# Scaling softmax probabilities: one broadcast product for two heads in place of two per-head products

## The chip, the cores and the metric

The kernel runs on one core of a Trainium2 chip. Its engines are TensorE (PE in the profile; PEld is its weight load), VectorE (DVE), ScalarE (ACT), GpSimd (POOL) and SyncE (SP, which here issues the DMAs). The metric is the device time of one execution in microseconds. Before the change the median of three runs is 2153.99 us, the lowest 2150.99, the highest 2158.84.

## The reference

One layer of a hybrid decoder runs over a prompt of 2048 tokens and a sample group of 8 x 8 tokens, with shared weights. What matters here is the attention of the prompt: 8 query heads on 2 key/value heads (so 4 heads in a group), head size 64, a causal window of 128, and a learned logit per head (the sink) that only enters the denominator.

```python
s = jnp.einsum('...qhgd,...shd->...hgqs', q, k) * (HEAD_DIM ** -0.5)
s = jnp.where(mask, s, NEG)
m = jnp.maximum(jnp.max(s, axis=-1, keepdims=True), sink)
e = jnp.exp(s - m)
pr = e / (jnp.sum(e, axis=-1, keepdims=True) + jnp.exp(sink - m))
return jnp.einsum('...hgqs,...shd->...qhgd', pr.astype(v.dtype), v)
```

The rest of the layer is an input projection, a pooling mixer, an output projection, a feed-forward block of width 4096 and a gated embedding. The change touches only the division that makes `pr`.

## The kernel before

The prompt is cut into 16 tiles of 128 tokens, and the sample group is one more tile of 64 (t = -1). The program has four parts, one after the other on TensorE: the attention part (projection, attention, pooling per tile), the output projection, the up projection, and the down projection with the gate. The attention part ends some 410 us into the span.

In the attention part, one loop over t weaves four generators in an order that is written out as a string of letters: `f` is `front` of tile t+1 (three projections, PSUM tiles `kvps`, `qps` and `ups`, then rotary embedding and transposes `trk` and `trq` of keys and queries), `a` is `attention` of tile t, `p` is `pooling` of tile t (transpose `tru`, products `pq`), `l` is `finish` of tile t-1 (`pss`), and `e` carries side work. At the last tile, t = 15, there is no next front; there `e` is `mixed.first`, which loads the output weights `wo` and starts the output projection (PSUM tile `pab`) so that TensorE has something between the steps of the last attention.

This weaving is the program order. The compiling layer then orders each engine's instructions anew from the dependencies and its own modelled durations (`schedule_with_timeline_sim=True`), unless a line holds an instruction to program order. So an edit of one instruction's kind or length can also move others, on all engines. Within an engine, instructions run in the order that results; an instruction that waits holds up everything behind it on its engine.

For a tile, `attention` (L491) goes through the two groups g of four heads:

- TensorE makes the scores of each head (`sc`, L505 and L506, two products each, 256 keys wide; 128 for tile 0).
- VectorE adds the mask, takes the running minimum of the negated scores and evicts them to `pr` (L509), a head at a time.
- ScalarE takes the exponential of each head in place, with its sum (L520).
- A short chain on four columns makes the denominators and their reciprocals `es` (L529 VectorE, L530 ScalarE, L531 and L532 VectorE).
- Four products scale the four heads in place: heads 0 and 2 on VectorE (L537), heads 1 and 3 on ScalarE (L535). Each takes one head of 128 x 256 and a per-partition scalar `es[:, hh:hh+1]`.
- TensorE transposes the four scaled heads of each block of 128 keys into one PSUM bank (`trp`, L547, four transposes). ScalarE casts the bank to `pt` (L549), VectorE writes the remainder of the cast beside it (L130, tile `pt`), and TensorE multiplies both with the values (`po`, L557 and L558).
- VectorE folds the two halves of `po` into `mix` (L560 and L561) and ScalarE squares them (L564).

The PSUM pool `tr` has two buffers. All of `trp`, `trk`, `trq` and `tru` take turns in them, and a transpose can start only when the reader of the tile two turns earlier is done. For `trp` the last reader is the remainder on VectorE, for the others a copy or cast on ScalarE (L460, L471, L581).

Of the kernel before, what the change touches and what calls it, by code (L numbers as in the profile page):

```python
# [14 lines left out]
ALU = mybir.AluOpType  # L15
PSUM = bass.MemoryType.PSUM

P = 128
# [70 lines left out]
def trunk(ctx: ExitStack, tc: tile.TileContext, i: dict, o: dict):  # L89
    nc = tc.nc  # L90
    V, A, G, T, SY = nc.vector, nc.scalar, nc.gpsimd, nc.tensor, nc.sync
# [37 lines left out]
    def lo_of(out, full, hi, eng=V):  # L129
        eng.tensor_tensor(out=out, in0=full, in1=hi.bitcast(F32), op=ALU.subtract)  # L130
# [143 lines left out]
    with ExitStack() as sa:  # L274
# [8 lines left out]
        op = sa.enter_context(tc.tile_pool(name="op", bufs=2, space=PSUM))  # L283
# [207 lines left out]
        def attention(t, kp, qT, mix, sq):  # L491

            nk = 1 if t == 0 else 2
            k0 = 256 - nk * P
            nkey = nk * P
            prs = []
            for g in range(2):
                pr = over.pool.tile([P, 4, 256], F32, tag="pr", bufs=2, name="pr")
                nm = over.pool.tile([P, 4], F32, tag="nm", bufs=2, name="nm")
                sm = over.pool.tile([P, 4], F32, tag="sm", bufs=2, name="sm")  # L500
                for h2 in range(2):
                    sc = scp.tile([P, 2, 256], F32, tag="sc", name="sc")
                    for e in range(2):
                        h = g * 4 + h2 * 2 + e
                        T.matmul(sc[:, e, :nkey], qT[:, h], kp[:, g * 2, k0:], start=True, stop=False)  # L505
                        T.matmul(sc[:, e, :nkey], qT[:, h], kp[:, g * 2 + 1, k0:], start=False, stop=True)  # L506
                    for e in range(2):
                        hh = h2 * 2 + e
                        V.tensor_tensor_reduce(  # L509
                            out=pr[:, hh, :nkey],  # L510
                            in0=sc[:, e, :nkey],
                            in1=ct[:, C_MASK + k0 : C_MASK + 256],
                            scale=-(HD**-0.5),
                            scalar=nsink[:, g * 4 + hh : g * 4 + hh + 1],
                            op0=ALU.add,
                            op1=ALU.min,
                            accum_out=nm[:, hh : hh + 1],
                        )
                for hh in range(4):
                    A.activation(  # L520
                        out=pr[:, hh, :nkey],
                        in_=pr[:, hh, :nkey],
                        func=AF.Exp,
                        scale=-1.0,
                        bias=nm[:, hh : hh + 1],
                        accum_out=sm[:, hh : hh + 1],
                    )
                es = over.pool.tile([P, 4], F32, tag="es", bufs=2, name="es")
                V.tensor_tensor(out=es, in0=nm, in1=sinkb[:, g * 4 : g * 4 + 4], op=ALU.add)  # L529
                A.activation(out=es, in_=es, func=AF.Exp)  # L530
                V.tensor_tensor(out=es, in0=es, in1=sm, op=ALU.add)  # L531
                V.reciprocal(es, es)  # L532
                for hh in range(4):
                    if hh % 2:
                        A.mul(out=pr[:, hh, :nkey], in_=pr[:, hh, :nkey], mul=es[:, hh : hh + 1])  # L535
                    else:
                        V.tensor_scalar_mul(pr[:, hh, :nkey], pr[:, hh, :nkey], es[:, hh : hh + 1])  # L537
                prs.append(pr)
                yield
            part = over.pool.tile([P, 4, P], F32, tag="part", bufs=1, name="part")  # L540
            for g in range(2):
                pr = prs[g]
                pts = []
                for kb in range(nk):
                    ps = tr.tile([P, 4, P], F32, tag="tr", name="trp")
                    for hh in range(4):
                        T.transpose(ps[:, hh, :], pr[:, hh, kb * P : (kb + 1) * P], ident)  # L547
                    pt = over.pool.tile([P, 2, 4, P], F32R, tag="pt", bufs=3, name="pt")
                    A.copy(out=pt[:, 0], in_=ps)  # L549
                    lo_of(pt[:, 1], ps, pt[:, 0])  # L550
                    pts.append(pt)
                yield

                po = op.tile([P, 4, P], F32, tag="o", name="po")
                for kb in range(nk):
                    vp = vps[(t - nk + 1 + kb) % 4]
                    T.matmul(po, vp[:, 2 * g : 2 * g + 2].rearrange("p a d -> p (a d)"), pts[kb][:, 0], start=kb == 0, stop=False)  # L557
                    T.matmul(po, vp[:, 4 + g : 6 + g].rearrange("p a d -> p (a d)"), pts[kb][:, 1], start=False, stop=kb == nk - 1)  # L558
                own, other = slice(g * HD, g * HD + HD), slice(HD - g * HD, 2 * HD - g * HD)
                V.tensor_copy(part[own], po[other])  # L560
                V.tensor_tensor(out=mix[own, 0:4, :], in0=po[own], in1=part[own], op=ALU.add)  # L561
                if g == 0:
                    yield
            A.activation(out=sq[:, 0:4, :], in_=mix[:, 0:4, :], func=AF.Square)  # L564
# [219 lines left out]
        for t in range(-1, NT):  # L784
            kr, vr, qr, u, kp, qT = res[t]
            if t + 1 < NT and t >= 0:
                split_head(t + 1)
            mix = pa.tile([P, 8, P], F32, tag="mix", bufs=2, name="mix")
            sq = pa.tile([P, 8, P], F32, tag="sq", bufs=2, name="sq")
            if t + 2 < NT:  # L790
                heads[t + 2] = head(t + 2)
            f = front(t + 1, *heads[t + 1], res[t + 1]) if t + 1 < NT else iter(())
            p = pooling(t, u, mix, sq)
            if t < 0:
                a = sample_attention(kr, vr, qr, mix, sq)
                for c in ORDER0.split():
                    next({"a": a, "p": p, "f": f}[c], None)
                run(a, p, finish(t, mix, sq))
                over_s.__exit__(None, None, None)
                over.pool = sa.enter_context(tc.tile_pool(name="over_p", bufs=1, side="right", reuse_waits="tile"))  # L800
                run(f)
            else:
                e = split_w_out((t - 3) % 4, (t - 3) // 4) if 3 <= t < 11 else iter(())
                if t == NT - 1:
                    sw.close()
                    s2 = ctx.enter_context(ExitStack())
                    mixed = Mixed(s2)
                    bank = sw.enter_context(tc.tile_pool(name="first", bufs=2, space=PSUM, reuse_waits="tile"))
                    e = mixed.first(bank)
                order = {NT - 2: ORDER1, NT - 1: ORDER2}.get(t, ORDERW if 3 <= t < 11 else ORDER)  # L810
                weave(order, a=attention(t, kp, qT, mix, sq), p=p, f=f, l=last, e=e)
                last = finish(t, mix, sq)
# [700 lines left out]
```

## Time and profile before

| | |
|---|---|
| runs (three) | 2150.99 to 2158.84 us, median 2153.99 |
| profiled execution | 2156.64 us, its span 2154.9 us |
| busy share of the span | PE 99%, PEld 87%, DVE 73%, ACT 44%, POOL 27% |
| mean granted TensorE clock | 0.996 |
| scaling on VectorE (L537) | 64 instructions, 26.1 us busy |
| scaling on ScalarE (L535) | 64 instructions, 28.6 us busy |

The profile comes from one execution. A row of the grouped view gives the line, the engine, the operation, what it writes and reads, how often, the busy time in us and the mean duration in ns, and then how long its engine stood idle just before it and who ended that. The waits view sums who waited for whom. In the view by windows each row is a stretch: its bounds, its length, and for PE, PEld, DVE, ACT and POOL the busy us with the number of instructions, then the granted TensorE clock, the DMA share and GB/s. A row of the timeline begins with the start in us and the time taken; two instructions that follow each other on an engine can overlap, so what one costs its engine in a stream is the distance between starts.

### The profile page before, as it was taken

To read this page: it belongs to the slowest core of one execution; us is meant where nothing else is said; L and a number is where in the kernel's file an instruction comes from. 1 tells how busy PE (TensorE), PEld (TensorE's weight loads), DVE (VectorE), ACT (ScalarE), POOL (GpSimd) and SP (SyncE) were. 2 spreads that over 40 slices of the span, in tenths; PEclk is the share of its full clock that TensorE was granted. 3 is DMA by queue.
4 is the path that set the end of the run, shared out by engine and by line. 5 is a ranking of instruction groups with operands and counts; after the bars stand their busy time and mean duration, and the time that the engine had idled before them with its cause. 6 is when DMAs were issued, how large, how long until landed. Compare 5 with 4: busy or idle time off the path is not lost. (4 is left out here: it accounts for less than half of the span.)

```text
span 2154.9 us, 31214 instructions
## 1 busy us (share of the span) xinstructions
PE 2129.8 (99%) x11439; PEld 1882.8 (87%) x11439; DVE 1573.8 (73%) x2719; ACT 956.8 (44%) x1864; POOL 576.3 (27%) x643
## 2 busy tenths in 40 slices
PE   8999999999999999999999999999999999999999
PEld 6888888788889999999999988788888888888887
DVE  6899888876688777555755566788888888876553
ACT  5676666545455445444544455233232233232221
POOL 2334343343440000000000035534534544300000
PEclk9999999999999999999999999999999999999999
DMA  7552122768789668666766532231231222342211
GB/s 221 176 174 92 63 70 67 264 220 249 230 259 322 223 217 273 208 191 190 225 197 189 164 111 92 97 101 49 92 99 53 97 91 72 107 138 83 89 54 40
DMA packets 310007, 320.43 MB, mean 149 GB/s; under 512 B 79775, under 2 KB 257247, under 8 KB 302654
## 3 DMA queue, kind: packets, MB, share of 16 engines
q1 hardware_dynamic: 309854, 318.44, 46.7%
q8 instruction: 90, 1.47, 0.3%
q14 instruction: 63, 0.52, 0.1%
HBM read 217.17 MB, written 102.51 MB: 148 GB/s over the span
## 5 line engine op out<-in xcount | busy, mean ns | idle before, releaser
L1278 DVE TENSOR_TENSOR z<-dn,z 128x512 f32<-128x512 f32 x416 | 277.8, 684 | 78.0 <-PE dn L1270 70.1
L130 DVE TENSOR_TENSOR g<-raw,g 128x512 fp32r<-128x512 f32 x336 | 226.8, 694 | 88.9 <-ACT g L207 88.2
L1052 PE MATMUL up<-e,g 128*128 128x352 f32 x832 | 269.5, 324 | 6.0 <-ACT snap L1059 5.8
L1053 PE MATMUL up<-e,g 128*128 128x352 f32 x832 | 267.9, 322 | 0.0
L1054 PE MATMUL up<-e,g 128*128 128x352 f32 x832 | 264.3, 323 | 0.0
L1217 POOL TENSOR_TENSOR raws<-raws 128x1024 f32<-128x1024 f32 x32 | 84.0, 2635 | 617.6 <-DVE wr L130 408.4
L207 ACT CAST g<-raw 128x512 fp32r<-128x512 f32 x336 | 203.8, 623 | 97.4 <-PE up L1054 77.4
L1268 PE MATMUL dn<-wr,ms 128*128 128x512 f32 x512 | 199.3, 390 | 1.5 <-DVE z L1278 1.5
L1269 PE MATMUL dn<-wr,ms 128*128 128x512 f32 x512 | 199.2, 389 | 0.0
L1270 PE MATMUL dn<-wr,ms 128*128 128x512 f32 x512 | 198.2, 389 | 0.0
L1052 PEld LDWEIGHTS up<-e,g 128*128 128x128 f32 x832 | 156.6, 188 | 7.2 <-ACT snap L1059 6.6
L1053 PEld LDWEIGHTS up<-e,g 128*128 128x128 f32 x832 | 157.4, 189 | 0.1
L1054 PEld LDWEIGHTS up<-e,g 128*128 128x128 f32 x832 | 156.0, 189 | 0.0
L1066 DVE TENSOR_TENSOR t<-up,snap 128x352 f32<-128x352 f32 x144 | 71.2, 520 | 115.4 <-ACT snap L1059 100.0
L207 ACT CAST m<-fr 128x512 fp32r<-128x512 f32 (+1 forms) x128 | 65.4, 514 | 194.2 <-PE dn L1270 172.5
L1268 PE MATMUL dn<-wr,m 128*128 128x512 f32 x384 | 149.5, 389 | 1.7 <-DVE z L1278 1.7
L1269 PE MATMUL dn<-wr,m 128*128 128x512 f32 x384 | 149.4, 389 | 0.0
L1270 PE MATMUL dn<-wr,m 128*128 128x512 f32 x384 | 149.3, 389 | 0.0
L848 POOL TENSOR_TENSOR s<-fr 128x256 f32<-128x256 f32 x64 | 54.1, 845 | 308.3 <-DVE ms L130 241.7
L1059 ACT COPY snap<-up 128x352 f32<-128x352 f32 x144 | 61.0, 454 | 165.6 <-PE up L1054 165.6
L207 ACT CAST wr<-raws 128x1024 fp32r<-128x1024 f32 x66 | 69.1, 1050 | 116.5 <-PE dn L1270 57.8
L1268 PEld LDWEIGHTS dn<-wr,ms 128*128 128x128 f32 x512 | 96.1, 188 | 22.1 <-issue 1.9
(279 smaller groups left out, 5725.8 us busy)
## 6 DMA issues: line engine op xcount, KB each, us to landing
raw<-in_w_up_dram SPq DMA_DIRECT2D x160, 256.0 KB, 4.4
raw<-upt SPq DMA_DIRECT2D x32, 1024.0 KB, 7.8
fr<-ffd SPq DMA_DIRECT2D x64, 512.0 KB, 3.5
ffd<-r SPq DMA_DIRECT2D x96, 256.0 KB, 2.9
upt<-raw SPq DMA_DIRECT2D x16, 1024.0 KB, 8.5
raws<-in_w_down_dram SPq DMA_DIRECT2D x32, 512.0 KB, 5.4
sp<-hfd SPq DMA_DIRECT2D x21, 704.0 KB, 6.6
xt<-in_x_t_dram SPq DMA_DIRECT2D x16, 512.0 KB, 5.7
```

The source lines that it names most:

```text
L130: eng.tensor_tensor(out=out, in0=full, in1=hi.bitcast(F32), op=ALU.subtract)
L207: copy(out=dst[:, 0], in_=src)
L1052: T.matmul(ps, l[0], r[0], start=st, stop=False, skip_group_check=not fresh)
L1053: T.matmul(ps, l[0], r[1], start=False, stop=False, skip_group_check=not fresh)
L1054: T.matmul(ps, l[1], r[0], start=False, stop=c == 3, skip_group_check=not fresh)
L1059: A.copy(out=s, in_=ps)
L1066: V.tensor_tensor(out=t, in0=ps, in1=s, op=ALU.add)
L1217: G.tensor_tensor(out=t, in0=x, in1=y, op=ALU.subtract)
L1268: T.matmul(ps, l[0], r[0], start=fresh and j == 0, stop=False, skip_group_check=not fresh)
L1269: T.matmul(ps, l[0], r[1], start=False, stop=False, skip_group_check=not fresh)
L1270: T.matmul(ps, l[1], r[0], start=False, stop=j == 1, skip_group_check=not fresh)
L1278: V.tensor_tensor(out=z, in0=ps, in1=z, op=ALU.add)
```

## The change

The loop over four heads with alternating engines is replaced. Heads 0 and 1 are scaled by a single elementwise product on VectorE, of a 128 x 2 x 256 block with the two reciprocals broadcast along the keys. Heads 2 and 3 are scaled on ScalarE, each as before with a per-partition scalar.

```diff
                 V.reciprocal(es, es)
-                for hh in range(4):
-                    if hh % 2:
-                        A.mul(out=pr[:, hh, :nkey], in_=pr[:, hh, :nkey], mul=es[:, hh : hh + 1])
-                    else:
-                        V.tensor_scalar_mul(pr[:, hh, :nkey], pr[:, hh, :nkey], es[:, hh : hh + 1])
+                some = pr[:, 0:2, :nkey]
+                V.tensor_tensor(out=some, in0=some, in1=es[:, 0:2].unsqueeze(2).to_broadcast([P, 2, nkey]), op=ALU.mult)
+                for hh in range(2, 4):
+                    A.mul(out=pr[:, hh, :nkey], in_=pr[:, hh, :nkey], mul=es[:, hh : hh + 1])
                 prs.append(pr)
```

The changed file is one line shorter, so from the transposes on each line number is one less than before (L547 becomes L546, and so on); the new product is L534 and the products on ScalarE are L536.

The order of the instructions is moved on every engine from tile 0 on, to the middle of the output projection; behind that it stands as before. Three places are shown.

VectorE, tile 4, second group of heads, before (`es` are the reciprocals, `qr` and `rb` the rotary embedding of tile 5's queries):

```order
L532 RECIPROCAL es<-es 128x4
L406 TENSOR_TENSOR qr<-qps,cs 128x512
L537 TENSOR_SCALAR pr<-pr,es 128x256 x2
L409 TENSOR_TENSOR rb<-qps,cs 128x8x32 x2
L373 TENSOR_SCALAR cs<-cs,rsq 128x128
```

and now:

```order
L532 RECIPROCAL es<-es 128x4
L534 TENSOR_TENSOR pr<-pr,es 128x512
L406 TENSOR_TENSOR qr<-qps,cs 128x512
L409 TENSOR_TENSOR rb<-qps,cs 128x8x32 x2
L373 TENSOR_SCALAR cs<-cs,rsq 128x128
```

Two instructions have become one, and it stands ahead of the rotary embedding's first product instead of behind it.

TensorE, from the last scores of tile 14 on, before (`trp` x8 are the transposes of tile 14's first group of heads, `trk` and `trq` those of tile 15's keys and queries):

```order
L506 MATMUL sc<-kp,qT 128x256
L580 MATMUL tru<-ident,u 128x128 x4
L547 MATMUL trp<-ident,pr 128x128 x8
L459 MATMUL trk<-identr,khl 128x128 x4
L470 MATMUL trq<-identr,qhl 128x128 x8
L547 MATMUL trp<-ident,pr 128x128
```

and now:

```order
L506 MATMUL sc<-kp,qT 128x256
L546 MATMUL trp<-ident,pr 128x128 x8
L631 MATMUL pss<-small,sq 128x1 x2
L556 MATMUL po<-pt,vp_136 128x512
L459 MATMUL trk<-identr,khl 128x128 x4
L557 MATMUL po<-pt,vp_136 128x512
L556 MATMUL po<-pt,vp_138 128x512
L470 MATMUL trq<-identr,qhl 128x128 x4
L557 MATMUL po<-pt,vp_138 128x512
L470 MATMUL trq<-identr,qhl 128x128 x4
L134 MATMUL pab<-wo,ms 128x512
```

The transposes of tile 14's first group now stand right behind the scores of its second group, the transposes of tile 15's keys and queries have products with the values between them, and the output projection (`pab`) begins right behind, ahead of tile 15's scores.

ScalarE, tile 14, the exponentials of the first group and what follows, before:

```order
L520 ACTIVATE pr,sm<-pr,nm 128x256 x3
L530 ACTIVATE es<-es 128x4
L474 ACTIVATE u<-ups,rsq 128x512
L535 ACTIVATE pr<-pr,es 128x256 x2
L621 COPY mix<-pq 128x512
```

and now, from the third exponential of that group on:

```order
L520 ACTIVATE pr,sm<-pr,nm 128x256
L580 COPY ux<-tru 128x4x128
L520 ACTIVATE pr,sm<-pr,nm 128x256
L530 ACTIVATE es<-es 128x4
L520 ACTIVATE pr,sm<-pr,nm 128x256 x4
L563 ACTIVATE sq<-mix 128x512
L530 ACTIVATE es<-es 128x4
L536 ACTIVATE pr<-pr,es 128x256 x4
L548 CAST pt<-trp 128x512 x2
```

The first group's scaling now stands behind the four exponentials of the second group, and both groups' scaling in one run ahead of the casts.

## The prediction

> **What bounds the kernel now.** I read the view by windows first, since the scaling products run only in the attention part, then the waits of TensorE in that part, then the timeline of its last 21 us. These are the attention part from the second tile on, the last two tiles, and the output projection:
>
> ```profile
> 66.00:385.00 319.00, 318.77 (x2007) 281.92 (x2006) 287.17 (x821) 214.98 (x565) 126.84 (x161) 1.00 0.33 107
> 385.00:406.00 21.00, 17.48 (x109) 15.53 (x108) 17.84 (x53) 17.35 (x48) 8.69 (x9) 0.84 0.91 353
> 406.00:600.00 194.00, 193.04 (x922) 158.93 (x921) 131.20 (x136) 96.94 (x160) 81.96 (x99) 1.00 0.72 224
> ```
>
> From 66 to 385 us TensorE is busy for 318.77 of 319.00 us. VectorE comes next with 287.17 (90%), ScalarE has 67%. Only in the stretch from 385 to 406 us is TensorE idle to speak of (3.5 us), and there its granted clock drops to 0.84.
>
> A busy TensorE need not be a TensorE at its pace, since its ends are modelled. So I compare starts. Two neighbours in the attention part, and two in the down projection:
>
> ```profile
> 180.14 0.39 PE L134 MATMUL ups<-wi,hT 128*128 128x512 f32 x1
> 180.37 0.39 PE L135 MATMUL ups<-wi,hT 128*128 128x512 f32 x1
> ...
> 1500.01 0.39 PE L1269 MATMUL dn<-wr,ms 128*128 128x512 f32 x1
> 1500.24 0.39 PE L1270 MATMUL dn<-wr,ms 128*128 128x512 f32 x1
> ```
>
> Both are 0.23 us apart, at the same width. The attention part therefore issues its products at the pace of a part that has nothing else to wait for. The waits of TensorE from 66 to 385 us, all of them:
>
> ```profile
> PE po L558 <- DVE pt L130: 0.2, 1, 0.2
> ```
>
> Not one transpose waits for a scaled head there. That is the main reading: the time of the edited step is hidden behind TensorE except in the last two tiles, where the front of the next tile is missing and the steps of one tile follow each other bare:
>
> ```profile
> PE trk L459 <- DVE pt L130: 1.3, 1, 1.3
> ...
> PE trp L547 <- ACT ux L581: 0.7, 1, 0.7
> PE trq L470 <- DVE pt L130: 0.7, 1, 0.7
> PE trp L547 <- ACT pr L535: 0.7, 1, 0.7
> ```
>
> Together 3.4 us, of which 0.7 us is a wait for scaling.
>
> The Trainium skill, page "Perfetto Trace Analysis", section "Identifying the Most-Contended Engine", says that the matmul's busy share is no measure of how near TensorE is to its limit, and to look at the weight loads' share instead. Here that share is 281.92 of 319 us, 88%, so by this rule an eighth of the stretch could still be hidden waiting; the equal distance of starts says that it is not, and I keep this as a rival below.
>
> **The change, part by part.** *VectorE, the product.* Removed are two scalings of a head, 64 instructions in all. Added are 32 products of 128 x 512. What a scaling and its nearest relatives cost:
>
> ```profile
> L537 DVE TENSOR_SCALAR pr<-pr,es x57: 277/351/1312, 67.8 to 385.0; 128x256 f32<-128x256 f32 x53, 128x128 f32<-128x128 f32 x4
> ...
> L406 DVE TENSOR_TENSOR qr<-qps,cs x15: 653/677/692, 66.4 to 376.9; 128x512 f32<-128x512 f32 x15
> ...
> L130 DVE TENSOR_TENSOR hT<-xt,hT x26: 675/684/1471, 76.6 to 354.0; 128x512 fp32r<-128x512 f32 x26
> ...
> L446 DVE CAST qhl<-qr x15: 405/426/731, 72.0 to 379.6; 128x512 fp32r<-128x512 f32 x15
> 384.97 0.62 DVE L537 TENSOR_SCALAR pr<-pr,es 128x256 f32<-128x256 f32 x2
> ```
>
> Each row has the shortest, median and longest duration in ns. A pair of scalings takes 0.62 us. A two-operand product of this kind with a broadcast operand is not in place in this trace, but L406 has a broadcast second operand (median 677 ns) and L130 both operands in SBUF (684 ns). I take 0.68 us. The bounds: from below the one-operand cast of the same size, 0.41 us; from above 0.70 us undisturbed and 1.47 us when it is held up. So one pair becomes 0.06 us dearer (-0.21 to +0.08 undisturbed), over 32 groups +2 us of VectorE (-7 to +3). Fewer instructions do not mean less time here. From 66 to 385 us this lies under TensorE's 318.77 us and costs 0. If that cover were gone, it would be the 2 us.
>
> *VectorE against GpSimd.* The long ends of those rows are instructions that overlap one on GpSimd:
>
> ```profile
> 162.64 1.50 DVE L537 TENSOR_SCALAR pr<-pr,es 128x256 f32<-128x256 f32 x2
> 162.70 0.91 ACT L535 ACTIVATE pr<-pr,es 128x256 f32<-128x256 f32 x2
> 162.75 1.23 POOL L595 TENSOR_TENSOR us<-ux 128x568 f32<-128x568 f32 x1
> ...
> 164.93 0.27 PE L547 MATMUL trp<-ident,pr 128*128 128x128 f32 x1
> ```
>
> The pair takes 1.50 us where 0.62 would do, and ends (164.14) just behind GpSimd's sum (163.98). With one instruction instead of two there is one occasion for this in place of two, but L130's 1471 ns shows that a product of two SBUF operands is held up too. Gain and loss stay below 0.9 us for a group. What waits behind the product is rotary embedding, the remainder of `pt`, and then the transposes: here they start 0.8 us after the scaling has ended, and by the waits above no group came too late. I cost it at nothing.
>
> *ScalarE* keeps two scalings per group (0.91 us a pair, above). Only which heads it takes is changed. The fourth head was ready at the end of ScalarE's pair and still is. The first transpose needs its head at 0.68 instead of 0.35 us; the wait counts to the last head, so 0.
>
> *The order.* Up to tile 13 the new orders swap neighbours. In the excerpt for tile 4 the product stands one place earlier than the pair did. Counting TensorE's instructions between a group's last score and its first transpose, I find none up to tile 13 that is nearer by more than 1.2 us, and that one is 15 us away; the near ones are as they were. I cost that at 0, with 0 to +3 us as its range (a single wait like the 0.7 us above in four tiles).
>
> *The last two tiles* do change. Before, the transposes of tile 14's first group came 2 us after its scaling had ended:
>
> ```profile
> 385.68 0.90 ACT L535 ACTIVATE pr<-pr,es 128x256 f32<-128x256 f32 x2
> ...
> 388.54 0.60 PE L547 MATMUL trp<-ident,pr 128*128 128x128 f32 x4
> ```
>
> In the new order of ScalarE this scaling stands behind the second group's four exponentials, and on TensorE the transposes stand right behind the second group's scores. Their durations:
>
> ```profile
> L509 DVE CUSTOM_DVE_ANT_0 pr<-sc,ct,nsink x128: 339/478/487, 63.1 to 403.3; 128x256 f32<-128x256 f32 x120, 128x128 f32<-128x128 f32 x8
> ...
> L520 ACT ACTIVATE pr<-pr,nm x128: 385/502/540, 64.2 to 405.5; 128x256 f32<-128x256 f32 x120, 128x128 f32<-128x128 f32 x8
> ...
> L564 ACT ACTIVATE sq<-mix x16: 617/631/647, 90.0 to 425.7; 128x512 f32<-128x512 f32 x16
> ...
> L530 ACT ACTIVATE es<-es x32: 188/205/213, 65.7 to 407.3; 128x4 f32<-128x4 f32 x32
> ...
> L549 ACT CAST pt<-trp x54: 564/587/617, 74.4 to 382.3; 128x512 fp32r<-128x512 f32 x54
> 387.63 0.28 PE L505 MATMUL sc<-kp,qT 128*128 128x256 f32 x1
> 387.75 0.28 PE L506 MATMUL sc<-kp,qT 128*128 128x256 f32 x1
> ...
> 409.42 1.03 PE L547 MATMUL trp<-ident,pr 128*128 128x128 f32 x8
> ```
>
> Counted from the first of these scores: the first exponential can start after a score (0.3 us) and an eviction (0.5); four exponentials 2.2, one square 0.6, the small exponential 0.2, two scalings 0.9, in all 4.7 us. The scores take 1.2 us (eight at 0.12 and a product of 0.23 between them). So TensorE waits 3.5 us where it waited 0.7 us: +2.8. Behind the transposes (1.0 us for eight) it waits for the first cast, which now stands behind the second group's scaling: 0.9 + 0.6 - 1.0 = 0.5 us more. In return, the keys' and queries' transposes have products with the values between them, and the output projection comes ahead of tile 15's scores: of the waits of 1.3, 0.7 and 0.7 us I let somewhat under half stand, 1.1 us, an estimate. Sum: 3.5 + 0.5 + 1.1 = 5.1 us against 3.4, +1.7. Against it stands that before, the instructions behind the waits ran at the reduced clock (0.84 over 21 us, 3.4 us of clock lost), and now part of that time is waiting anyway: I take off 0.7 us, a fifth. That leaves **+1 us**, with -3 to +5 as its range.
>
> The sum, against the profiled execution of 2156.6 us (span 2154.9 and 1.8 around it): 2156.6 + 0 + 1 = 2157.6. That execution lies 2.6 us above the median of the runs, 2154.0. On the scale of the median I forecast **2155 us**, no change that can be told: about 0.5%, 10.8 us, is what a measurement of this kernel can tell from no change (the three runs spread over 7.8 us).
>
> **The rivals.** *The last two tiles close up.* The output projection, moved ahead, could fill every gap. Then 3.5 us of idle time and 3.4 us of lost clock go: 2147. For it: in the new order `pab` follows the transposes of the queries at once. Against it: ScalarE's order delays the first group's scaling before that. Even this ends within 0.5%, since the whole loss to be won there is 6.9 us.
>
> *The clock stays low for longer.* A longer gap costs 3.4 us of clock once more: 2158. The Trainium skill, page "TensorE: Matmul & The Clock Gate", section "HAM oscillation — how this bites in real kernels", warns of idle gaps of more than about 3.4 us; the new gap of 3.5 us is such a one. The trace agrees only in part: its clock fell to 0.84 with no wait longer than 1.34 us, so the penalty was there already.
>
> *VectorE sets the pace* (the slower side). VectorE has 31.8 us to spare from 66 to 385 us. If the broadcast product were held up by GpSimd in nearly every group, up to 1.47 us against the pair's 0.62, 28 groups would take 24 us, and VectorE would be as full as TensorE. Then transposes come late from the point where a product ends more than the 0.8 us after the old pair that tile 4's first group had to spare. At 0.6 us of wait per group this is 17 us: 2171. For it: the product reads two SBUF operands, and L130 reached 1471 ns. Against it: L130's median in 26 instructions is 684 ns, so hold-ups are rare, and GpSimd is busy for only 40% of the stretch.
>
> *TensorE was not at its limit.* By the page on traces above, VectorE's 2 us would count in full: 2157, inside the likeliest case's own range. The edit then does not do what its words promise, as VectorE's work grows.
>
> **How the numbers follow.** My forecast has 0.73 (its own range 2150 to 2160), the closed gap 0.10, the longer low clock with TensorE's hidden waits 0.10, VectorE's pace 0.07. The range of 2147 to 2162 leaves out most of the last case and a little at both ends. Slower by over 0.5% (above 2165) is VectorE's pace with 0.05 of its 0.07; faster by over 0.5% (below 2143) has no mechanism here and gets 0.02 for what I did not see; within 0.5% gets 0.93.
>
> **What would show it.** In the new profile: L534 with a median near 0.68 us, 32 times; VectorE's busy time from 66 to 385 us within 3 us of 287; TensorE's waits there below 1 us in total and no row of `trp` among them; between 385 and 406 us a wait of about 3.5 us of `trp` L546 for ScalarE or VectorE, `trk` and `trq` waits that are shorter, and the clock below 1. The forecast is wrong if `trp` waits for `pr` in the tiles before 14, if L534 is far from 0.68 us, or if the clock falls in a stretch where it did not before.

## The result: slower by 0.6%, more than half of it lost behind the attention part

The changed kernel takes 2167.53 us (median of 6 runs, 2167.07 to 2172.17), the kernel before 2154.44 in the same comparison. The ratio is 1.0059, with a 95% interval from 1.0049 to 1.0069: about 13 us slower. The forecast was 2155 in a range of 2147 to 2162, with 0.05 for slower. It was wrong. The profiled execution took 2167.33 us with a span of 2165.5.

The three stretches of the prediction in the view by windows, now after the change (bounds, length, busy us of PE, PEld, DVE, ACT and POOL, then the granted clock):

```profile
66.00:385.00 319.00, 316.28 (x1980) 279.32 (x1978) 284.33 (x772) 210.73 (x552) 129.80 (x160) 0.99 0.33 107
385.00:406.00 21.00, 15.79 (x93) 13.74 (x92) 18.16 (x48) 15.05 (x39) 7.05 (x8) 0.76 0.95 372
406.00:600.00 194.00, 187.86 (x906) 153.64 (x905) 125.46 (x142) 93.97 (x164) 72.00 (x94) 1.00 0.70 214
```

TensorE has lost 2.5 us of busy time in the attention part, 1.7 in the last two tiles, and 5.2 in the output projection (187.86 against 193.04), which the prediction gave no term at all. What TensorE waits for, in the attention part up to 385 us:

```profile
PE ups L134 <- DVE es L532: 2.1, 1, 2.1
PE trq L470 <- DVE pt L130: 0.6, 1, 0.6
```

and from 385 to 606 us:

```profile
PE trp L546 <- DVE pr L534: 4.5, 1, 4.5
PE pab L134 <- ACT z L252: 4.1, 5, 1.9
PE pss L631 <- POOL sq L627: 1.5, 2, 0.8
PE trx L887 <- DVE ez L877: 0.9, 1, 0.9
PE trx L887 <- DVE z L877: 0.4, 1, 0.4
```

The last four rows are new but for 0.5 us. Before the change `trx` and `pss` did not wait there at all, and `pab` had this one wait:

```profile
PE pab L134 <- ACT z L252: 0.5, 1, 0.5
```

Because the orders differ, the k-th product of one kernel isn't the k-th of the other. But there are places at which TensorE has issued the same set of instructions in both. I compare the start of the next one there, worked out from both traces:

| place (us before the change) | after minus before, us | step |
|---|---|---|
| 57, tile 0 | -3.0 | -3.0 |
| 126, tile 3 | -2.5 | +0.5 |
| 148, tile 4 | -0.1 | +2.3 |
| 152 | +1.6 | +1.7 |
| 385, behind the first scores of tile 14 | +0.9 | -0.7 |
| 388.5, transposes of tile 14 | +5.5 | +4.6 |
| 408, 19th `pab` | +2.9 | -2.6 |
| 430 | +2.2 | -0.7 |
| 447, first `trx` after the change | +4.3 | +2.1 |
| 482 | +6.6 | +2.3 |
| 517 | +8.7 | +2.1 |
| 605, end of the output projection | +9.3 | +0.6 |
| 2125, last part | +10.7 | +1.4 |

The first step is the clock alone (shown at the end). The largest lasting loss is the 7.1 us between 430 and 605 us; from 57 to 385 us, in the attention part, it is 3.9 us. The two profiled executions differ by 10.7 us and the medians by 13, since the one of before was 2.2 us above its median and the other 0.2 us below.

**Where the loss in the output projection starts.** SyncE's issues around 430 us, before the change:

```profile
429.60 0.60 SPq L230 DMA_DIRECT2D mr<-mixd  x1
430.28 0.61 SPq L178 DMA_DIRECT2D g_post_mix<-in_g_post_mix_dram  x1
...
434.76 0.33 SPq L230 DMA_DIRECT2D mr<-mixd  x1
```

and after:

```profile
430.78 0.60 SPq L230 DMA_DIRECT2D mr<-mixd  x1
432.23 0.33 SPq L636 DMA_DIRECT2D mixd<-mix  x1
436.95 0.32 SPq L230 DMA_DIRECT2D mr<-mixd  x1
437.36 0.38 SPq L178 DMA_DIRECT2D g_post_mix<-in_g_post_mix_dram  x1
```

The order of SyncE's instructions says what was swapped (`mixd_80` is the sample group, `mixd_85` tile 4). Before:

```
L637 DMA mixd_96<-mix 128x1024
L230 DMA mr<-mixd_80 128x8x64
L178 DMA g_post_mix<-in_g_post_mix_dram 128x1024
L178 DMA g_pre_mlp<-in_g_pre_mlp_dram 128x1024
L872 DMA xt<-in_x_prompt_dram 128x1024 x2
L230 DMA mr<-mixd_85 128x1024
```

After:

```
L230 DMA mr<-mixd_80 128x8x64
L636 DMA mixd_96<-mix 128x1024
L230 DMA mr<-mixd_85 128x1024
L178 DMA g_post_mix<-in_g_post_mix_dram 128x1024
L178 DMA g_pre_mlp<-in_g_pre_mlp_dram 128x1024
L872 DMA xt<-in_x_prompt_dram 128x1024 x2
```

The load of `mr` for tile 4 now stands ahead of the two gain rows. It is needed late, but there are only two `mr` buffers, so it cannot be issued until VectorE has made the remainder of an earlier one; and SyncE issues nothing behind it meanwhile. On VectorE after the change:

```profile
435.70 1.22 DVE L130 TENSOR_TENSOR ms<-mr,ms 128x1024 fp32r<-128x1024 f32 x1 [0.26 <-ACT ms L207]
...
443.70 1.28 DVE L873 SCALAR_TENSOR_TENSOR ez<-ez,rsq,g_post_mix 128x1024 f32<-128x1024 f32 x1 [6.71 <-DMA g_post_mix<-in_g_post_mix_dram]
```

The remainder ends at 436.92, the load goes out at 436.95, the gain row 7.1 us later than before, and the first residual starts at 443.70. Before the change:

```profile
436.08 1.29 DVE L874 SCALAR_TENSOR_TENSOR ez<-ez,rsq,g_post_mix 128x1024 f32<-128x1024 f32 x1 [1.35 <-POOL rsq L143]
```

The chain of residuals is 7.6 us late. It goes through VectorE, ScalarE and GpSimd tile by tile (its first nine scalings L877, in the order in which they run, are 7.5, 7.5, 8.0, 11.9, 6.7, 7.6, 8.5, 8.5 and 8.9 us later than before) and does not catch up. TensorE runs into it in steps of about 2 us, at `trx` and at `pab`.

### The profile page after: what moved, and what is told of

Same layout as the page of the kernel before. It is cut to its first block, busy times and chain, and to the rows that moved or that the text cites. A ratio compares the mean times of both kernels' runs of the same rounds, so it can differ in the third digit from the quotient of the medians.

```text
span 2165.5 us, 31175 instructions
## 1 busy us (share of the span) xinstructions
PE 2131.2 (98%) x11439; PEld 1881.7 (87%) x11439; DVE 1575.9 (73%) x2687; ACT 955.9 (44%) x1864; POOL 574.2 (27%) x643
## 4 chain that ended last, share of the span: by engine, by line
PE 81%; DVE 6%; DMA 4%; POOL 3%; issue 3%; ACT 2%; SPq 0%; ACTq 0%; DVEq 0%; POOLq 0%
PE dn L1267 9%; PE dn L1269 9%; PE dn L1268 9%; PE up L1051 9%; PE up L1053 9%; PE up L1052 9%; PE pg L136 3%; PE pg L135 3%; PE pg L134 3%; PE ups L134 1%; PE ups L136 1%; PE ups L135 1%; DMA raw<-in_w_up_dram 1%; PE trp L546 1%; PE qps L136 1%
## 5 line engine op out<-in xcount | busy, mean ns | idle before, releaser
L207 ACT CAST wr<-raws 128x1024 fp32r<-128x1024 f32 x66 | 69.2, 1051 | 117.7 <-PE dn L1269 57.8
L141 POOL TENSOR_SCALAR rst<-ss 128x1 f32<-128x1 f32 (+1 forms) x68 | 22.4, 330 | 358.9 <-ACT ms L183 211.5
```

The source lines that it names most:

```text
L207: copy(out=dst[:, 0], in_=src)
```

## The experiments

Theories: *queue* (the late gain row), *product* (the new product or the heads' new assignment), *order* (how the scheduler arranged the rest), *clock*. All ratios are to the kernel before, run in the same comparison.

| run | median us | ratio, 95% interval |
|---|---|---|
| the change | 2167.53 | 1.0059 (1.0049 to 1.0069) |
| 1 change, gain rows first | 2160.17 | 1.0026 (1.0018 to 1.0035) |
| 2 before, gain rows late | 2160.56 | 1.0024 (1.0012 to 1.0035) |
| 3 change in tiles 14 and 15 alone | 2154.92 | 0.9998 (0.9988 to 1.0008) |
| 4 change in tiles 0 to 13 alone | 2167.39 | 1.0059 (1.0044 to 1.0073) |
| 5 heads reassigned, no product | 2165.10 | 1.0045 (1.0033 to 1.0058) |
| 6 as 5, gain rows first | 2159.41 | 1.0025 (1.0015 to 1.0034) |
| 7 product on heads 0 and 2, gain rows first | 2158.70 | 1.0019 (1.0010 to 1.0028) |
| 8 as 1, tile 14 scaled first | 2165.36 | 1.0048 (1.0034 to 1.0063) |
| 9 as 1, scores of tile 14 covered | 2162.76 | 1.0038 (1.0026 to 1.0050) |
| 10 before, first `snap` early | 2160.77 | 1.0027 (1.0016 to 1.0038) |
| 11 as 9, first `snap` early | 2169.15 | 1.0069 (1.0056 to 1.0083) |
| 12 the change in the old order | 2154.89 | 0.9997 (0.9989 to 1.0006) |
| 13 the old step in the new order | 2166.03 | 1.0048 (1.0035 to 1.0060) |

Edges are added between instructions of one engine; an edge itself sets an order and waits for nothing else. But the layer orders all engines anew around it, so such a kernel differs from the one that it was made from in more places than the edge names. Comparing the two orders in the traces tells in how many, and the text gives it where it matters. Added lines shift line numbers by a few. The excerpts are shortened; in those of runs 2 and 10 `kind` stands for the same value as in run 12.

### 1 and 2: the gain rows, first and late

```diff
 def load(self, t):
-    SY.dma_start(raw[:, :, :n], mixd[t])
+    with tc.issue_after(gain_loads[-1].ins) if t == 4 else nullcontext():
+        SY.dma_start(raw[:, :, :n], mixd[t])
```

> The changed kernel, with one edge more: SyncE issues the load of mr for tile 4 behind the loads of the two gain rows, as it stood before the change. The attention part is in the changed order on every engine. Queue theory (the loss arises because g_post_mix is issued 7.1 us later, behind a load that waits for a free mr buffer): VectorE no longer waits 6.7 us for g_post_mix, TensorE's lateness stops growing between 440 and 606 us (it grew by 6.2 us there), and the time is about 2161 us, 6 to 7 us below the changed kernel's 2167.5. Attention theory (the edited step and the last two tiles cost it): 2167, as the attention part is unchanged. Clock theory (the half clock falls in another place): 2167, with no change in the output projection's waits.

In run 2 the same edge stands the other way round, in the kernel before: both gain loads are held behind tile 4's load.

```diff
-    SY.dma_start(raw[:, :, :n], mixd[t])
+    mr = SY.dma_start(raw[:, :, :n], mixd[t])
+    if t == 4:
+        for g in gain_loads:
+            tc.add_manual_dep(g.ins, mr.ins.name, kind, reason="gains_late")
```

> The kernel before, with the two gain rows issued behind tile 4's load of mr, as in the changed kernel; nothing in the attention part differs from the kernel before. Queue theory: VectorE waits some 5 to 7 us for g_post_mix, the chain of the residuals starts that much later, and the time rises by 5 to 8 us, to 2160 to 2162. Attention theory and clock theory: no change, 2154.

Run 1, SyncE, and TensorE's waits from 385 to 606 us:

```profile
431.52 0.60 SPq L233 DMA_DIRECT2D mr<-mixd  x1
432.97 0.33 SPq L639 DMA_DIRECT2D mixd<-mix  x1
433.39 0.38 SPq L180 DMA_DIRECT2D g_post_mix<-in_g_post_mix_dram  x1
```

```profile
PE trp L549 <- DVE pr L537: 4.5, 1, 4.5
PE pss L634 <- POOL sq L630: 1.5, 2, 0.8
PE pab L134 <- ACT z L255: 0.3, 1, 0.3
```

The gain row is out 4.0 us earlier than in the changed kernel, `pab` waits 0.3 instead of 4.1 us, `trx` not at all, and the time falls by 7.4 us. TensorE's lateness, 3.9 us at 432 us, is 3.6 us at the first product of the up projection, so it no longer grows there. Besides tile 4's load, few instructions stand elsewhere than in the changed kernel (TensorE 2, VectorE 8, ScalarE 3, GpSimd 2, SyncE 5), all of them behind the swap. Run 2, SyncE, and then what VectorE and TensorE wait for:

```profile
433.72 0.33 SPq L232 DMA_DIRECT2D mr<-mixd  x1
434.10 0.43 SPq L180 DMA_DIRECT2D g_post_mix<-in_g_post_mix_dram  x1
```

```profile
DVE ez L884 <- DMA g_post_mix<-in_g_post_mix_dram: 2.5, 1, 2.5
```

```profile
PE pab L134 <- ACT z L262: 2.7, 3, 2.4
PE pab L134 <- DVE z L264: 1.3, 1, 1.3
```

VectorE waits 2.5 us for the row, less than expected, since here the buffer came free 3.2 us earlier; the time still rises by 5.9 us (2.6 to 7.5 by the interval). So two places in one queue, with nothing of the change, make a kernel slower, together with what moved behind them: from 436 us on 24 of TensorE's instructions and 12 of VectorE's stand elsewhere than before the change. How much of the 5.9 us is the late row alone is not shown. The queue theory holds: the swap, with the moves that it brings, is worth 7.4 and 5.9 us. Left over are 5.5 us.

### 3 and 4: the change in some tiles only

```diff
+if t >= NT - 2:
+    some = pr[:, 0:2, :nkey]
...
+else:
+    for hh in range(4):
...
```

Run 4 has `t < NT - 2` there.

> The change made for tiles 14 and 15 alone. SyncE's order is the one of the kernel before, with the gain rows ahead of tile 4's load. Queue theory: only what the end of the attention part costs, 0 to 3 us, so 2154 to 2157. If the last two tiles cause the loss (a longer wait of their transposes, or the clock behind it): 2163 to 2168.

> The change made for tiles 0 to 13 alone; tiles 14 and 15 as before. SyncE's order is the one of the changed kernel, with the gain rows behind tile 4's load. Queue theory: nothing lost from 66 to 385 us, 5 to 9 us lost in the output projection, 2160 to 2166. If the broadcast product itself costs time in the steady part: lateness that grows from tile to tile there, at 0.1 to 0.5 us a group. If only the last two tiles matter: 2154.

Run 3 costs nothing, run 4 everything. But run 3 also kept nearly the whole old order (11 of TensorE's instructions stand elsewhere), and run 4 nearly the whole new one (5). Run 4 came 1.4 us above the upper end expected by the queue theory. Its tiles 14 and 15 hold the old step, and yet its transposes of tile 14 wait as long as the changed kernel's: 4.4 us in all, 4.1 the longest.

```profile
PE trp L553 <- DVE pr L543: 4.4, 2, 4.1
```

So this wait doesn't come from the step in the tile in which it stands. It comes with an order that was settled by edits further ahead.

### 5, 6 and 7: heads without product, product without heads

Run 5 keeps per-head scalings, heads 0 and 1 on VectorE, 2 and 3 on ScalarE; run 6 adds the edge of run 1. Run 7 has the product on heads 0 and 2 with that edge.

```diff
 for hh in range(4):
-    if hh % 2:
+    if hh > 1:
```

and for run 7

```diff
+some = pr.rearrange("p (a b) k -> p b a k", b=2)[:, 0, :, :nkey]
+V.tensor_tensor(out=some, in0=some, in1=es.rearrange("p (a b) -> p b a", b=2)[:, 0].unsqueeze(2).to_broadcast([P, 2, nkey]), op=ALU.mult)
+for hh in (1, 3):
```

> No broadcast product: heads 0 and 1 are scaled on VectorE one by one, heads 2 and 3 on ScalarE; only the assignment of heads differs from the kernel before. SyncE's order has the gain rows behind tile 4's load, as in the changed kernel. Queue theory: the output projection loses 5 to 8 us although no product is in the kernel, so 2160 to 2168. If the broadcast product is what costs: 2154.

> The kernel with only the heads reassigned, and tile 4's load of mr behind the gain rows; the attention part is in the same order as in that kernel. Queue theory: 5 to 8 us below it, as with the changed kernel (7.4 us). What is then left over the kernel before is the order of the attention part: 0 to 6 us. Otherwise: the same time as with the heads reassigned alone.

> The broadcast product, but on heads 0 and 2, so that ScalarE keeps heads 1 and 3 as before; the gain rows are ahead of tile 4's load. If the product costs time by itself, it costs here what it costs in the changed kernel with the gain rows first: 2160. If that kernel's remaining 5.5 us are only the order that the reassigned heads brought: 2154 to 2157.

What TensorE waits for at `pab`, in run 5 and then in run 6:

```profile
PE pab L134 <- ACT z L252: 3.5, 4, 1.7
```

```profile
PE pab L134 <- ACT z L255: 1.2, 2, 0.7
```

Most of the loss is there with no product in the kernel (2165.1), and the edge takes 5.7 us of it away. Run 7 came out at 2158.7, between the two expectations: it didn't tell product and order apart.

### 8 and 9: two edges for the 4.5 us at tile 14

In run 8 the exponentials of tile 14's second group are held behind the first group's scaling, on ScalarE.

```diff
 for hh in range(4):
+    with tc.issue_after(scaled.ins) if t == NT - 2 and g else nullcontext():
         A.activation(
```

In run 9 the last half of tile 15's `ups` products is held behind the first group's scores, on TensorE.

```diff
+late = t == NT - 1 and c0 == 768 and k >= 4
+with tc.issue_after(state["scores"]) if late else nullcontext():
     mm3(ps[:n, :cw], ...)
```

> The changed kernel with the gain rows first, and for tile 14 one more edge: the exponentials of the second group of heads stand on ScalarE behind the scaling of the first group. Tail theory (the transposes of tile 14's first group wait 4.5 us because its scaling stands behind the second group's exponentials): that wait falls below 1.5 us, and the time falls by 2 to 3 us from 2160.2 to 2157 to 2158. Otherwise the wait only moves to the second group's transposes: 2160.

> The changed kernel with the gain rows first, and the last 12 of tile 15's 24 ups products on TensorE held behind the scores of tile 14's first group, so that they cover its softmax as they do in the kernel before. Cover theory (in the changed order these scores come after the last ups product, so nothing covers the chain to the first transpose): the wait of 4.5 us at these transposes falls below 1.5 us, and the time falls by 2 to 3 us against the 2160.2 of the kernel with the gain rows alone moved, to 2157 to 2158. If VectorE or ScalarE only hand the wait on to later steps of the tail: 2160.

Run 8:

```profile
PE trp L550 <- DVE pr L538: 4.4, 1, 4.4
```

The wait stayed, for its releaser is VectorE. The median rose by 5.2 us, though the two intervals touch; the profiled execution, at 2160.8 us the fastest of five, doesn't show where. In run 9 the wait went, and others came:

```profile
PE trk L464 <- DVE pt L130: 1.5, 1, 1.5
PE trp L553 <- ACT ux L587: 1.0, 1, 1.0
PE trq L475 <- ACT kp L465: 0.7, 1, 0.7
PE pab L136 <- DVE ms L130: 0.7, 1, 0.7
...
PE trp L553 <- DVE pr L541: 0.4, 1, 0.4
```

Run 9's execution came into the last tiles 2.0 us behind run 1's, most of it by 3.4 us of half clock from 37 us on (more on that clock at the end). Counted from there it is 4.6 us ahead at the transposes and 1.3 us at the 19th `pab`, and at 622 us nothing is left of it. So the covered scores do take the wait away, but the time doesn't fall, and the edge moved much else (132 of TensorE's instructions, 67 of VectorE's). Neither theory of a single wait in the tail gave a faster kernel.

### 10 and 11: the wait at the start of the up projection

All kernels so far wait there for ScalarE's copy of a PSUM bank, as here before the change:

```profile
PE up L1052 <- ACT snap L1059: 4.3, 1, 4.3
```

The copy stands behind a square that waits 5.3 us for VectorE. Run 10 holds that square behind the copy; run 11 does so on top of run 9.

```diff
+first = A.copy(out=s, in_=ps)
+if stalled:
+    tc.add_manual_dep(stalled.pop().ins, first.ins.name, kind, reason="snap_first")
```

> The kernel before, its attention part and output projection untouched; at the start of the up projection the first copy of an up bank (snap) stands on ScalarE ahead of the square of tile 13's residual, which waits 5.3 us for VectorE. TensorE waited 4.3 us there for that copy, in all kernels so far. If ScalarE's order is the cause of that wait too: it falls below 1.5 us, and the time falls by 3 to 4 us, to 2151. If the wait then comes from the next late step of the residuals: 2154.

> The changed kernel with all three edges: the gain rows first, the scores of tile 14 covered, the first snap ahead of tile 13's square. If the three losses are separate, it lies 3 to 4 us below the kernel with the first two edges, and within 0.3% of the kernel before: 2152 to 2156.

Run 10, TensorE's waits from 606 us on:

```profile
PE up L1058 <- DVE g L130: 3.4, 2, 2.9
PE up L1056 <- ACT snap L1063: 2.4, 2, 2.2
...
PE up L1056 <- DVE z L256: 0.8, 1, 0.8
```

At 621 us TensorE was 3.0 us ahead of the kernel before, at 669 us 4.7 us behind it. Waits of 6.6 us stand where one of 4.3 us stood, and the time rose. What the copy alone is worth isn't shown, for the edge moved far more than the square: between 598 and 731 us 468 of TensorE's instructions, 97 of VectorE's and 35 of ScalarE's stand elsewhere. Run 11 shows the same: 2169.2, some 6 us above run 9 where 3 to 4 below were expected. No version came out ahead of the kernel before.

### 12 and 13: edit and order crossed

Here every engine's instructions are held, one behind the other, in a given order up to the middle of the output projection. A table of places in program order is added, and this, once the program is written down:

```diff
+for a, b in zip(order, order[1:]):
+    tc.add_manual_dep(here[b], here[a].name, kind, reason="pin")
```

With it TensorE, ScalarE, GpSimd and SyncE of run 12 stand instruction by instruction as before the change, and VectorE too, but for one product where two scalings were. Run 13 is the reverse.

> The changed kernel (broadcast product on heads 0 and 1, ScalarE on heads 2 and 3), with each engine's instructions held in the order of the kernel before up to the middle of the output projection: the product stands where the second of the two per-head products stood, everything else in its old place. Order theory (the change costs nothing by itself; all 13 us come from the order that the scheduler made of it): 2154 to 2156. Product theory (the product, or the heads' new assignment, costs the 5.5 us that are left with the gain rows first): 2159 to 2161.

> The kernel before (four per-head products, ScalarE on heads 1 and 3), with each engine's instructions held in the order of the changed kernel: the two per-head products stand where the broadcast product stood. Order theory: the whole loss without the change, 2166 to 2169. Product theory: 5 us less, 2161 to 2163.

Run 12 in the attention part:

```profile
66.00:385.00 319.00, 319.00 (x2009) 282.41 (x2009) 288.13 (x790) 216.39 (x571) 130.90 (x162) 1.00 0.33 107
```

Run 13, VectorE's wait for the gain row and two of TensorE's:

```profile
DVE ez L1001 <- DMA g_post_mix<-in_g_post_mix_dram: 6.9, 1, 6.9
```

```profile
PE trp L674 <- DVE pr L664: 4.1, 1, 4.1
PE pab L261 <- ACT z L379: 3.5, 4, 1.5
```

The change in the old order costs nothing (-0.1 us, at most 1.3 by the interval). The old step in the new order costs 11 us (7.5 to 12.9), with the same waits as the change. That is the cause, shown from both sides: **the loss is the order, some 6 to 7 us of it (7.4, 5.9 and 5.7 in three pairs) one swap in SyncE's queue with the few moves behind it, and the edit itself is free in the old order.** Between the 11 us of the old step and the 13 us of the change in the new order the intervals do not tell a difference. Why the scheduler swapped these loads no trace tells. Left open is also the split of the other 5 us between its places: runs 8 and 9 did not lower their sum, and runs 5 and 7, with other orders again, lose time without the wait of `ups` at 148 us.

## Why the prediction was wrong, step by step

**The product: right.** All 32 of them:

```profile
L534 DVE TENSOR_TENSOR pr<-pr,es x32: 409/691/886, 64.5 to 419.5; 128x512 f32<-128x512 f32 x30, 128x256 f32<-128x256 f32 x2
```

The median is 691 ns where 0.68 us was said. In the same order (run 12) VectorE grew by 1.0 us of busy time (+2, -7 to +3 predicted), and TensorE's cover hid it. From the page "Perfetto Trace Analysis" of the Trainium skill, section "Identifying the Most-Contended Engine", I had drawn a rival in which VectorE's extra work counts in full. Run 12's time alone can't rule out 1.0 us (-2.4 to +1.3 by the interval), but its starts can: from the same product to the same product, 58.6 to 385 us, TensorE takes 325.7 us where it took 326.3, and it waits for nothing. A weight-load share below 100% doesn't mean hidden waiting here: it is 89% in this stretch (282.41 of 319 us), and 82% from 1500 to 1600 us in the down projection before the change, where the products follow each other at the same 0.23 us.

**The order up to tile 13: a term of 0 that was mis-sized, with +3 as its upper end; it measured 2.7 us** by the two waits from 66 to 385 us, and 3.9 us by the starts from 57 to 385 us, 1.7 us of it by half clock behind the larger wait. I had counted only the distance from scores to transposes. The larger wait is of another kind. After the change, around 148 us:

```profile
144.42 1.78 DVE L761 SCALAR_TENSOR_TENSOR wsp<-wraw,gains,wsp 128x512 fp32r<-128x512 f32 x1
...
147.52 0.34 DVE L432 SCALAR_TENSOR_TENSOR vp<-kvps,rsq,vp 128x128 fp32r<-128x128 f32 x1
...
148.01 0.48 PE L134 MATMUL ups<-wi,hT 128*128 128x512 f32 x1 [2.09 <-DVE es L532]
```

`ups` takes the PSUM buffer of `kvps` (the pool `mmp` has two), and the last reader of that is L432, which ends at 147.86. It stands behind a split of output weights that took 1.78 us. The profile names the instruction after it, so this reading is by the code. My reading of VectorE, 90% over the attention part, was a mean: from 126 to 172 us, where the output weights are split, it was 94% before the change:

```profile
126.00:172.00 46.00, 45.77 (x286) 39.99 (x286) 43.22 (x116) 31.98 (x83) 19.96 (x23) 1.00 0.40 135
```

**The last two tiles: within the range, partly by luck.** At the 19th `pab` TensorE was 2.0 us later than at the scores (+1, -3 to +5 predicted), but the terms were off both ways. The wait of 3.5 us measured 4.5, and the clock of 0.76 instead of 0.84 over 21 us cost 1.7 us more where 0.7 us had been taken off; the 0.5 us for the first cast and the 1.1 us for `trk` and `trq` came to nothing. The releaser was VectorE's product, not ScalarE's scaling. The reason was not seen: in the old order 13 `ups` products came behind the first group's scores and covered the softmax, in the new one none.

**The output projection: the step that failed.** The sum was "2156.6 + 0 + 1", with no term for the stretch from 406 us on, although the order was known to be moved to the middle of it. I followed ScalarE, VectorE and TensorE at three places, all in the attention part, and never went through SyncE's queue. There a load that waits for a buffer had been put ahead of the gain rows: 6 to 7 us. The bounds had been drawn around the costed places, not around everything that was moved, and so the range ended at 2162. With the gain rows first (run 1) the same change takes 2160.2 us, inside it. Two of the prediction's own signs did show it wrong elsewhere: TensorE's waits up to 385 us were not below 1 us, and the clock fell in a new stretch, at 149 us.

**The rivals.** VectorE's pace (2171) is near the measured time, but for a wrong reason: VectorE is no busier (284.33 us), and run 5 has most of the loss without any product. By its own sum VectorE would have been busy for 311 of 319 us (287 + 24), not as full as TensorE. The tail did not close up. The longer low clock came to 1.7 us of the 3.4 us that it was priced at.

## What to carry to other kernels

When a scheduler orders the engines, an edit of one instruction can cost far from where it stands: go through the whole reach of the moved order, the DMA queue first, and ask of each issue what it waits for and what is queued behind it. Pin the old order under a new edit before judging the edit: here that separated a step that is free from an order that costs 0.5% (run 13). An added edge is no clean experiment by itself, since the scheduler moves other instructions around it: compare the whole order, as with run 10. Loads that a chain needs early, such as the gain rows, deserve an explicit edge ahead of loads that wait for a buffer (runs 1 and 6).

## What the chip showed unexpectedly

**The clock halves where TensorE was hardly idle, and not in every execution.** Before the change it did from 51.0 to 57.8 us, though TensorE's only wait from 30 to 51 us was 0.7 us, at 40.8 us. This stretch, and the same one of the changed kernel:

```profile
51.00:57.80 6.80, 6.80 (x36) 6.80 (x36) 0.36 (x1) 2.47 (x6) 1.94 (x4) 0.50 0.49 125
```

```profile
51.00:57.80 6.80, 6.80 (x52) 6.13 (x52) 2.92 (x9) 5.05 (x11) 2.72 (x5) 1.00 0.65 185
```

That is the step of -3.0 us at the head of the table. Run 12 has the order of the kernel before, and yet its clock fell where that kernel's did not. From 34 to 41 us, before the change and in run 12:

```profile
34.00:41.00 7.00, 6.34 (x48) 4.91 (x47) 6.18 (x26) 5.68 (x18) 4.58 (x7) 1.00 0.68 206
```

```profile
34.00:41.00 7.00, 7.00 (x39) 5.71 (x36) 5.43 (x23) 5.44 (x18) 4.66 (x7) 0.76 0.58 182
```

Except at the end of the span, the half clock came in stretches of 3.4, 6.8 or 10.2 us in all traces. By the starts of TensorE's instructions each 3.4 us of it cost 1.0 to 1.7 us, so single executions differ by what a small change is worth. The Trainium skill, page "TensorE: Matmul & The Clock Gate", section "HAM oscillation — how this bites in real kernels", looks to idle gaps for the cause. Behind the 2.1 us at 148 us the changed kernel had one (149.3 to 152.7, the +1.7 in the table):

```profile
149.30:152.70 3.40, 3.40 (x10) 2.52 (x9) 3.37 (x8) 2.34 (x5) 1.88 (x3) 0.50 0.03 11
```

So had run 11, which waited 2.0 us at that place (150.4 to 153.8). Runs 1, 4, 8, 9 and 13 waited 1.4 to 1.6 us there and had none.
